# Down product of three middle groups of the second FFN: 2x2 block products made of seven, with the partial outputs in HBM

## The chip, the cores and the metric

The kernel runs on one core of a Trainium2 chip. TensorE (PE) multiplies and writes its sums into PSUM, eight banks of 128 partitions by 512 float32. VectorE (DVE) and ScalarE (ACT) read PSUM and SBUF; GpSimd (POOL) computes on SBUF and issues transfers; SyncE (SP) issues transfers. Each engine works its own queue in order, and engines wait for each other by semaphores.

The metric is device time in microseconds (us). Before the change it is 884.45 us, the median of three runs (884.32 to 885.13).

## The reference

One decoder layer on 512 tokens of width 1024, all float32: a half-step SwiGLU feed-forward layer (FFN), a mixer of a gated recurrence and sliding-window attention, and a second FFN, each between two RMS norms. The change concerns the second FFN:

```python
def swiglu(x, w_gu, w_down):
    gate, up = jnp.split(x @ w_gu, 2, axis=-1)
    return (jax.nn.silu(gate) * up) @ w_down
...
    x = x + 0.5 * rms_norm(swiglu(rms_norm(x, ffn2_pre_g[l]), ffn2_w_gu[l], ffn2_w_down[l]), ffn2_post_g[l])
```

`w_gu` is 1024 x 5632 (gate and up, 2816 columns each) and `w_down` is 2816 x 1024.

## The kernel before

**Numbers.** To keep float32 accuracy, each operand of a product is split into a rounded high part (`F32R`) and the rest, the low part. A product is three matmuls: high x high, high x low, low x high. For a weight block, ACT casts the high part (`act.copy`) and DVE subtracts it from the block to get the low part (`dve.tensor_sub`). Such a pair of tiles is a *unit*.

**Weights.** The class `Weights` holds the list of all loads and units in the order in which PE uses them. Raw weights are loaded by SP into three rotating buffers of 1 MB (`NRAW`), and units go into six rotating pairs (`NWS`). `take()` is called when PE is about to use a unit; it first issues the low parts, and the next cast, of units up to four ahead (`AHEAD`), then runs whatever was put off with `later(n, ...)` to the n-th take from then. So the place of every ACT and DVE instruction in its queue follows from the order of the calls; the schedule is manual, and nothing reorders it. When the last unit of a raw buffer has been split, the next load is issued.

**The second FFN.** The 2816 hidden features are 22 blocks of 128, in the groups `GROUPS2` = (0, 6), (6, 10), (10, 14), (14, 18), (18, 22). For each group the hidden values are computed (gate and up products, SiLU, multiplication), and then the down product of that group, whose result is added to `parts`, eight tiles of 128 tokens x 512 output columns in SBUF. The first group's gate and up products are plain (`classic`). From block 6 on two blocks at a time are made by `quad`: gate and up weights and the halves of the input form 2x2 blocks, whose product is done with seven half-size products instead of eight (the weight combinations are made by DVE in place in the raw buffer, `combine` in `add_quad`; the input's were made once, in `Next.sums`). Each of the seven takes one unit and is 24 matmuls of 128x256. `quad` ends with a SiLU of the gate half (`g1`), a multiplication, and `low_parts`, which splits the hidden values into high and low.

**The down product before** (line 1430 on): for each half `dh` of the output columns and each block f of the group, four token blocks `tb` times three matmuls of 128x512 (`mm3_out`, L1425 to L1427): 96 matmuls per middle group, from four units of 1024 elements per partition. DVE then adds each of the eight banks into `parts` (L1446). In the first group ACT copies the banks into `parts` (L1444).

**The last group** is done token block by token block: its down product is added to `parts`, the squares are summed, and the post-norm and the residual follow (from L1464). POOL multiplies by the gain there (L1495). Between the first group's hidden values and this, POOL has no work.

**Buffers.** SBUF tiles of 2 KB per partition come from one pool of 44 (`t2k`), short-lived ones from a pool of 8 (`wt`), PSUM banks from a pool of 8. A tile that reuses a buffer waits for the last reader of the former one.

Of the kernel before, what the change touches and what calls it, by code (L numbers as in the profile page):

```python
# [32 lines left out]
CLASSIC1, CLASSIC2 = 4, 6  # L33
PUMPS = [(2, 1)] * 8 + [(1, 1), (1, 0), (4, 0)]
# [77 lines left out]
def tile_layer(ctx: ExitStack, tc: tile.TileContext, out: bass.AP, **ins: bass.AP):  # L112
# [8 lines left out]
    psum = ctx.enter_context(tc.tile_pool(name="psum", bufs=8, space=bass.MemoryType.PSUM))  # L121
    E = mybir.EngineType
# [3 lines left out]
    HALF = [slice(0, T // 2), slice(T // 2, T)]  # L126

# [3 lines left out]
    def t2k(name, dt=F32):  # L131
        return big.tile([P, T], dt, tag="t2k", name=name, bufs=NT2K)
# [140 lines left out]

    for f0, f1 in GROUPS2:
        for f in range(f0, f1, 2):
            (add_gate_up if f < CLASSIC2 else add_quad)(w2, f, "b")
        if f1 < FC:
            for dh in range(2):
                for f in range(f0, f1, 4):
                    add_down(f, min(4, f1 - f), dh)  # L280
        else:
            for f in range(f0, f1, 4):
                for dh in range(2):
                    add_down(f, min(4, f1 - f), dh)
# [353 lines left out]
    class Hidden:  # L638
# [24 lines left out]
        def quad(self, f, last, ahead):  # L663
# [3 lines left out]
            hs = [(t2k(f"hh{n}{j}", F32R), t2k(f"hl{n}{j}", F32R)) for j in range(2)]  # L667
# [10 lines left out]
            def low_parts(x, h):  # L678
                for j in range(2):
                    act.copy(hs[j][0][:, HALF[h]], x[:, HALF[j]])  # L680
                for j in range(2):
                    hh, hl = hs[j]
                    dve.tensor_sub(hl[:, HALF[h]], x[:, HALF[j]], hh.bitcast(F32)[:, HALF[h]])
# [5 lines left out]
            p1, p7, u2, u4, g1 = (wt(f"{s}{n}") for s in ("p1", "p7", "u2", "u4", "g1"))  # L689
            seven(A, "b11", True)  # L690
            act.copy(p1, A)
# [4 lines left out]
            seven(B, "b21", True)  # L696
            dve.tensor_add(p1, p1, B)  # L697
            W.later(1, act.activation, p1, p1, AF.Silu)
# [15 lines left out]
            for j in range(2):  # L714
                self.hs[f + j] = hs[j]
# [35 lines left out]
        def chunks(self, f0, f1, ahead=AHEAD):  # L751
            for f in range(f0, f1, 2):
                self.quad(f, f == f1 - 2, ahead if f == f1 - 2 else AHEAD)
            return [self.hs.pop(f) for f in range(f0, f1)]

# [673 lines left out]
    parts = {}  # L1429
    for g, (f0, f1) in enumerate(GROUPS2[:-1]):  # L1430
        hs = hid.chunks(f0, f1) if g else hid.classic(f1, banks, {3: [(n2.sums, 0)], 3.5: [(n2.lows, 0)], 4.5: [(n2.sums, 1)], 5: [(n2.lows, 1)]}, AHEAD - 1)
        for dh in range(2):
            ybanks = [bank(f"yb{g}{dh}{tb}") for tb in range(NB)]
            for f in range(f0, f1):
                if f % 2 == 0:
                    w = W.take()
                for tb in range(NB):
                    mm3_out(ybanks[tb], hs[f - f0], tb, w, f % 2, ALL, f == f0, f == f1 - 1)
                if g == 0 and (dh, f) in ((0, 0), (0, 2), (1, 2), (1, 4)):
                    (n2.sums if f == 2 * dh else n2.lows)(2 + dh)  # L1440
            for tb in range(NB):
                if g == 0:
                    parts[tb, dh] = t2k(f"yp_b{tb}{dh}")
                    act.copy(parts[tb, dh], ybanks[tb])  # L1444
                else:
                    dve.tensor_add(parts[tb, dh], ybanks[tb], parts[tb, dh])  # L1446
    f0, f1 = GROUPS2[-1]
    hs = hid.chunks(f0, f1, ahead=5)
# [15 lines left out]
    for tb in range(NB):  # L1464
# [8 lines left out]
        for i, f in steps:  # L1473
# [12 lines left out]
            if f == f1 - 1:  # L1486
                y = parts[tb, dh][:, c0:c1]
                dve.tensor_add(y, banks[i][:, :c1 - c0], y)
# [52 lines left out]
```

## Time and profile before

| what | us or share |
|---|---|
| runs, median of three | 884.45 |
| profiled execution | 886.26, span 884.6 from first to last instruction, granted clock 0.997 |
| PE busy | 873.8 (99%) |
| DVE, ACT, POOL busy | 668.5 (76%), 459.5 (52%), 129.0 (15%) |
| one middle group, gate and up products (626.20 to 666.50) | 40.30 |
| the same group's down product (666.50 to 688.29) | 21.79 |
| HBM read, written | 83.67 MB, 2.10 MB |

The profile is one execution, recorded by the hardware profiler. A group of instructions is shown as line, engine, operation, out<-in, partitions x elements, count, and then busy time, the mean duration in ns, and the idle time of the engine just before them with what ended it. The chain of waits follows the work that ended last back to what released each step. A timeline row is start, length, engine, line, operation. PE's durations overlap, since matmuls are pipelined: the spacing of their starts is what they cost. The same holds in a smaller degree for DVE and ACT.

### The profile page before, as it was taken

To read this page: it belongs to the slowest core of one execution; us is meant where nothing else is said; L and a number is where in the kernel's file an instruction comes from. 1 tells how busy PE (TensorE), PEld (TensorE's weight loads), DVE (VectorE), ACT (ScalarE), POOL (GpSimd) and SP (SyncE) were. 2 spreads that over 40 slices of the span, in tenths; PEclk is the share of its full clock that TensorE was granted. 3 is DMA by queue.
4 is the path that set the end of the run, shared out by engine and by line. 5 is a ranking of instruction groups with operands and counts; after the bars stand their busy time and mean duration, and the time that the engine had idled before them with its cause. 6 is when DMAs were issued, how large, how long until landed. Compare 5 with 4: busy or idle time off the path is not lost.

```text
span 884.6 us, 14243 instructions
## 1 busy us (share of the span) xinstructions
PE 873.8 (99%) x5768; PEld 801.5 (91%) x5768; DVE 668.5 (76%) x993; ACT 459.5 (52%) x791; POOL 129.0 (15%) x117
## 2 busy tenths in 40 slices
PE   8999999999999999999999999999999999999997
PEld 8988999989989998998887899888998998998996
DVE  4979758778778864889999679588677677777754
ACT  6646534544535554457787346535463452552542
POOL 2010000000000015435463154210000000000013
PEclk9999999999999999999999999999999999999999
DMA  7242243152242253332301130224232241261212
GB/s 240 73 152 83 92 142 103 54 162 72 73 142 97 84 167 96 96 96 76 115 1 49 60 131 5 93 95 143 96 127 65 96 145 46 96 190 37 86 46 96
DMA packets 83553, 86.68 MB, mean 98 GB/s; under 512 B 3664, under 2 KB 75680, under 8 KB 83488
## 3 DMA queue, kind: packets, MB, share of 16 engines
q1 hardware_dynamic: 83312, 85.64, 30.2%
q8 instruction: 45, 0.74, 0.3%
q14 instruction: 20, 0.16, 0.1%
q10 hardware_dynamic: 144, 0.13, 0.0%
q0 software_dynamic: 32, 0.00, 0.0%
HBM read 83.67 MB, written 2.10 MB: 97 GB/s over the span
## 4 chain that ended last, share of the span: by engine, by line
PE 91%; DVE 5%; ACT 2%; issue 1%; DMA 1%; POOL 0%; SPq 0%; POOLq 0%; DVEq 0%; ACTq 0%
PE aa L676 12%; PE ab L676 10%; PE da L676 6%; PE db L676 5%; PE ya L361 4%; PE ya L362 4%; PE ya L363 4%; PE yb L1426 4%; PE yb L1427 4%; PE yb L1425 4%; PE ba L676 3%; PE bb L676 3%; PE a_first L841 1%; PE an L380 1%; PE mn L380 1%; PE mn L387 1%
## 5 line engine op out<-in xcount | busy, mean ns | idle before, releaser
L361 PE MATMUL ya<-hha,whi_ad 128*128 128x512 f32 x158 | 61.5, 389 | 0.0
L362 PE MATMUL ya<-hla,whi_ad 128*128 128x512 f32 x158 | 61.5, 389 | 0.0
L363 PE MATMUL ya<-hha,wlo_ad 128*128 128x512 f32 x158 | 61.5, 389 | 0.0
L1425 PE MATMUL yb<-whi_bd,hhb 128*128 128x512 f32 x144 | 56.1, 389 | 0.0
L1426 PE MATMUL yb<-wlo_bd,hhb 128*128 128x512 f32 x144 | 56.1, 389 | 0.0
L1427 PE MATMUL yb<-whi_bd,hlb 128*128 128x512 f32 x144 | 56.0, 389 | 0.0
L1495 POOL TENSOR_TENSOR yp_b<-yp_b,grow 128x512 f32<-128x512 f32 (+1 forms) x8 | 9.7, 1222 | 282.0 <-ACT ysq L1489 282.0
L942 POOL MEMSET bd_w_rg<- 128x512 f32 x1 | 0.5, 528 | 266.0 <-PE aa L676 266.0
L363 PEld LDWEIGHTS ya<-hha,wlo_ad 128*128 128x128 f32 x158 | 29.7, 188 | 6.2
L361 PEld LDWEIGHTS ya<-hha,whi_ad 128*128 128x128 f32 x158 | 29.7, 188 | 6.1
L362 PEld LDWEIGHTS ya<-hla,whi_ad 128*128 128x128 f32 x158 | 29.7, 188 | 6.0
L1427 PEld LDWEIGHTS yb<-whi_bd,hlb 128*128 128x128 f32 x144 | 27.0, 188 | 5.6
L1425 PEld LDWEIGHTS yb<-whi_bd,hhb 128*128 128x128 f32 x144 | 27.0, 188 | 5.6
L1426 PEld LDWEIGHTS yb<-wlo_bd,hhb 128*128 128x128 f32 x144 | 27.0, 188 | 5.5
L176 DVE TENSOR_TENSOR wlo_bd<-raw_bd,whi_bd 128x1024 fp32r<-128x1024 f32 x22 | 26.4, 1219 | 3.6 <-ACT whi_bd L171 3.6
L171 ACT CAST whi_bd<-raw_bd 128x1024 fp32r<-128x1024 f32 x22 | 22.9, 1049 | 5.1 <-PE bb L676 3.8
L1446 DVE TENSOR_TENSOR yp_b<-yb,yp_b 128x512 f32<-128x512 f32 x24 | 16.4, 692 | 11.6 <-PE yb L1427 11.6
L1000 DVE TENSOR_TENSOR yp_a<-ya,yp_a 128x512 f32<-128x512 f32 x24 | 16.4, 686 | 8.8 <-PE ya L363 8.8
L697 DVE TENSOR_TENSOR p1a<-p1a,ba 128x512 f32<-128x512 f32 x9 | 6.2, 688 | 21.7 <-PE ba L676 21.7
L697 DVE TENSOR_TENSOR p1b<-p1b,bb 128x512 f32<-128x512 f32 x8 | 5.5, 688 | 18.2 <-PE bb L676 18.2
L380 PE MATMUL an<-xh_mx,whi_xl 128*128 128x256 f32 x64 | 15.9, 289 | 0.0
L381 PE MATMUL an<-xh_mx,wlo_xl 128*128 128x256 f32 x64 | 15.5, 283 | 0.0
(1523 smaller groups left out, 3418.4 us busy)
## 6 DMA issues: line engine op xcount, KB each, us to landing
raw_bd<-in_ffn_w_down SPq DMA_DIRECT2D x10, 1024.0 KB, 6.8
xn<-in_x SPq DMA_DIRECT2D x8, 256.0 KB, 4.6
raw_q<-in_w_in SPq DMA_DIRECT2D x4, 512.0 KB, 3.8
out_dram<-yp_b SPq DMA_DIRECT2D x7, 256.0 KB, 2.0
first<-in_ffn_w_gu SPq DMA_DIRECT2D x4, 256.0 KB, 5.1
raw_second<-in_ffn_w_gu SPq DMA_DIRECT2D x2, 512.0 KB
raw_ag__104<-in_ffn_w_gu SPq DMA_DIRECT2D x1, 1024.0 KB
raw_au__286<-in_ffn_w_gu SPq DMA_DIRECT2D x1, 1024.0 KB, 5.8
```

The source lines that it names most:

```text
L171: act.copy(two(hi, x), x)
L176: low.tensor_sub(two(lo, x), x, two(hi.bitcast(F32), x))
L361: pe.matmul(ps, hi[:, k, :], xh, start=start, stop=False)
L362: pe.matmul(ps, hi[:, k, :], xl, start=False, stop=False)
L363: pe.matmul(ps, lo[:, k, :], xh, start=False, stop=stop)
L380: pe.matmul(ps[:, sl], hi[:, k, :], xh, start=k == 0, stop=False)
L676: pe.matmul(o, w[:, k, js], x, start=first and i + j + k == 0, stop=k == 3 and i == 2, skip_group_check=True)
L1000: dve.tensor_add(parts[c], b, parts[c])
L1425: pe.matmul(ps, hh[:, blk], hi[:, k, cs], start=start, stop=False)
L1426: pe.matmul(ps, hh[:, blk], lo[:, k, cs], start=False, stop=False)
L1427: pe.matmul(ps, hl_[:, blk], hi[:, k, cs], start=False, stop=stop)
L1446: dve.tensor_add(parts[tb, dh], ybanks[tb], parts[tb, dh])
```

## The change

For the three middle groups, blocks 6 to 17 (`SEVEN_DOWN = 6, 18`), the down product is done with 2x2 blocks too. The hidden values of a group are 512 tokens x 512 features; the left factor's four blocks are token halves x feature pairs, the right factor's are feature pairs x column halves. Seven products of the blocks' sums and differences take the place of eight:

- *Weights* (`add_seven_down`): two loads of 1 MB with whole rows of `w_down`, and seven units of 1024 elements; four of them are combinations that DVE makes in place.
- *Hidden values* (`seven_left`, `seven_right`, `form`): instead of eight splits of 256 columns, seven forms of 512: blocks a11, a12, a22 and the combinations s1 to s4. The forms are made as soon as `quad` has the halves, some put off to later takes.
- *Products* (`seven_down`): seven times 12 matmuls of 128x512, 84 per group, in pairs of banks A, B, D, E. After the first product ACT copies A into B, and the third product accumulates on that copy.
- *Output* (`to_parts`): `parts` are now eight tiles in HBM. ACT copies a bank into a staging tile, and POOL issues a transfer that adds it to one or two of the parts: 12 copies and 14 transfers of 256 KB per group. The first group's result is copied to staging (negated for the right half) and stored by POOL. Before the last group's gate and up products POOL issues the loads of the eight parts into SBUF; the right half is subtracted at the end, since its sign is turned.
- *All quads*: bank A is copied by ACT into bank B, and the fourth product accumulates there, instead of a copy into `p1` and an addition by DVE.

```diff
+SEVEN_DOWN = 6, 18
...
+    def add_seven_down(f):
+        wd = ins["ffn2_w_down"]
+        rx, ry = (W.raw(lambda i=i: load_raw([wd[0, (f + i) * P:(f + i + 2) * P, :]], 2, D, f"b{'xy'[i // 2]}d{f}_")) for i in (0, 2))
+        left, right = HALF_D
+        b11, b12, b21, b22 = (rx, left), (rx, right), (ry, left), (ry, right)
...
+        unit(b11, "p")
+        unit(b12, "q", combine(dve.tensor_add, b12, b22, b12))
+        unit(b21, "r")
+        unit(b12, "s", combine(dve.tensor_add, b12, b12, b11))
+        unit(b21, "t", combine(dve.tensor_add, b21, b12, b21))
+        unit(b11, "u", combine(dve.tensor_sub, b11, b12, b22))
+        unit(b22, "v")
...
+        def form(self, name, x):
+            hh, hl = t2k(f"hh{name}", F32R), t2k(f"hl{name}", F32R)
+            act.copy(hh, x)
+            dve.tensor_sub(hl, x, hh.bitcast(F32))
+            self.forms[name] = hh, hl
+
+        def seven_left(self, f, x, second):
+            self.blocks[second, 0] = x
+            self.form("a12" if second else "a11", x)
+
+        def seven_right(self, f, x, second):
+            self.blocks[second, 1] = x
+            a11, a21 = self.blocks[0, 0], self.blocks[0, 1]
+            if not second:
+                s3 = wt(f"s3{self.name}{f}")
+                dve.tensor_sub(s3, a11, a21)
+                self.form("s3", s3)
+                return
+            a12, a22 = self.blocks[1, 0], x
+            s1, s2, s4 = (wt(f"{s}{self.name}{f}") for s in ("s1", "s2", "s4"))
+            dve.tensor_sub(s1, a22, a21)
+            dve.scalar_tensor_tensor(s2, s1, -1.0, a11, op0=ALU.mult, op1=ALU.subtract)
+            self.form("s2", s2)
+            W.later(1, self.form, "a22", a22)
+            W.later(2, self.form, "s1", s1)
+            W.later(3, dve.scalar_tensor_tensor, s4, s2, -1.0, a12, ALU.mult, ALU.subtract)
+            W.later(3, self.form, "s4", s4)
...
             seven(A, "b11", True)
-            act.copy(p1, A)
+            act.copy(B, A)
...
-            seven(B, "b21", True)
-            dve.tensor_add(p1, p1, B)
-            W.later(1, act.activation, p1, p1, AF.Silu)
+            seven(B, "b21", False)
+            W.later(1, act.activation, p1, B, AF.Silu)
...
+    parts = {(tb, dh): hbm.tile([P, T], F32, name=f"yp_b{tb}{dh}") for tb in range(NB) for dh in range(2)}
+
+    def seven_down(f):
+        forms = hid.seven_forms(f)
+        A, B, Dd, E_ = ([bank(f"y{s}{f}{i}") for i in range(2)] for s in "abde")
+
+        def seven(banks, form, first, stop):
+            w = hi, lo = W.take()
+            hh, hl_ = forms[form]
+            for i in range(2):
+                for k in range(2):
+                    js = slice(k * (T // 2) + i * P, k * (T // 2) + (i + 1) * P)
+                    pe.matmul(banks[i], hh[:, js], hi[:, k, :], start=first and k == 0, stop=False, skip_group_check=True)
+                    pe.matmul(banks[i], hh[:, js], lo[:, k, :], start=False, stop=False, skip_group_check=True)
+                    pe.matmul(banks[i], hl_[:, js], hi[:, k, :], start=False, stop=k == 1, skip_group_check=True)
+
+        def to_parts(banks, *blocks):
+            for i in range(2):
+                st = t2k("stage")
+                act.copy(st, banks[i])
+                for tb, dh in blocks:
+                    pool.dma_start(parts[2 * tb + i, dh], st, accum_op=ALU.add)
+
+        seven(A, "a11", True, True)
+        for i in range(2):
+            act.copy(B[i], A[i])
+        seven(Dd, "s3", True, True)
+        to_parts(Dd, (1, 1))
+        seven(B, "a12", False, True)
+        to_parts(B, (0, 0))
+        seven(A, "s2", False, True)
+        to_parts(A, (1, 0))
+        seven(Dd, "a22", False, True)
+        to_parts(Dd, (1, 0))
+        seven(A, "s1", False, True)
+        to_parts(A, (1, 1), (0, 1))
+        seven(E_, "s4", True, True)
+        to_parts(E_, (0, 1))
...
-                if g == 0:
-                    parts[tb, dh] = t2k(f"yp_b{tb}{dh}")
-                    act.copy(parts[tb, dh], ybanks[tb])
-                else:
-                    dve.tensor_add(parts[tb, dh], ybanks[tb], parts[tb, dh])
+                st = t2k("stage")
+                act.activation(st, ybanks[tb], AF.Copy, scale=-1.0 if dh else 1.0)
+                pool.dma_start(parts[tb, dh], st)
...
+    in_hbm, parts = parts, {}
+    for tb in range(NB):
+        for dh in range(2):
+            parts[tb, dh] = t2k(f"yp_b{tb}{dh}")
+            pool.dma_start(parts[tb, dh], in_hbm[tb, dh])
...
-                dve.tensor_add(y, banks[i][:, :c1 - c0], y)
+                (dve.tensor_sub if dh else dve.tensor_add)(y, banks[i][:, :c1 - c0], y)
```

## The prediction

> **What bounds the kernel now.** I read the page's busy shares and its chain first, then the stage table and the chain in order of time around the second group, then the timelines of ScalarE (ACT) and VectorE (DVE) where its down product begins. The page:
>
> ```profile
> PE 873.8 (99%) x5768; PEld 801.5 (91%) x5768; DVE 668.5 (76%) x993; ACT 459.5 (52%) x791; POOL 129.0 (15%) x117
> ...
> PE 91%; DVE 5%; ACT 2%; issue 1%; DMA 1%; POOL 0%; SPq 0%; POOLq 0%; DVEq 0%; ACTq 0%
> ...
> L176 DVE TENSOR_TENSOR wlo_bd<-raw_bd,whi_bd 128x1024 fp32r<-128x1024 f32 x22 | 26.4, 1219 | 3.6 <-ACT whi_bd L171 3.6
> L171 ACT CAST whi_bd<-raw_bd 128x1024 fp32r<-128x1024 f32 x22 | 22.9, 1049 | 5.1 <-PE bb L676 3.8
> L1446 DVE TENSOR_TENSOR yp_b<-yb,yp_b 128x512 f32<-128x512 f32 x24 | 16.4, 692 | 11.6 <-PE yb L1427 11.6
> ```
>
> TensorE (PE) is busy throughout and carries the chain; DVE follows at 76%. In the changed stages the margin is this (columns: stretch, length, busy time of PE, PEld, DVE, ACT, POOL, clock, DMA share, GB/s):
>
> ```profile
> 626.20:666.50 40.30, 40.30 (x337) 40.30 (x337) 27.42 (x32) 22.62 (x32) 0.00 (x0) 1.00 0.40 131
> 666.50:688.29 21.79, 21.79 (x99) 18.02 (x98) 15.92 (x20) 5.53 (x7) 0.00 (x0) 1.00 0.16 49
> ```
>
> One middle group is 14 gate/up products of 2.88 us, then 21.8 us of down product, with no hole in PE. A group takes 62.10 us (626.19 to 688.29), the same in all three, by the chain in order of time (start, length):
>
> ```profile
> 626.19 2.87 PE ab L676 x24
> ...
> 688.29 2.87 PE ab L676 x24
> ```
>  In the down stage ACT is nearly free. What matters is what stands at the seam:
>
> ```profile
> 663.66 0.69 DVE L703 TENSOR_TENSOR u2b<-u2b,db 128x512 f32<-128x512 f32 x1 [1.57 <-PE db L676]
> 664.38 0.69 DVE L704 TENSOR_TENSOR u2b<-p1b,u2b 128x512 f32<-128x512 f32 x1
> 664.99 1.22 DVE L176 TENSOR_TENSOR wlo_bd<-raw_bd,whi_bd 128x1024 fp32r<-128x1024 f32 x1
> ```
> ```profile
> 666.34 0.40 PE L1425 MATMUL yb<-whi_bd,hhb 128*128 128x512 f32 x1
> 666.58 0.40 PE L1426 MATMUL yb<-wlo_bd,hhb 128*128 128x512 f32 x1
> ```
> ```profile
> 666.54 0.60 ACT L707 ACTIVATE g1b<-ab 128x512 f32<-128x512 f32 x1 [0.72 <-PE ab L676]
> 667.90 0.72 ACT L680 CAST hhb<-g1b 128x256 fp32r<-128x256 f32 x2 [0.76 <-DVE g1b L686]
> 671.46 1.05 ACT L211 CAST whi_bq__7151<-raw_bx__7041 128x1024 fp32r<-128x1024 f32 x1 [2.84 <-DVE raw_bx__7041 L220]
> ```
>
> Here DVE's last work of the quad starts 0.2 us after PE ends its sixth product (663.46), and ACT's last SiLU 0.2 us after the seventh (666.34). The third line shows an ACT cast of a combined weight block: it stands idle until DVE's combination is done, and everything behind it in ACT's queue stands too.
>
> **Part 1, the matmuls.** 96 of 128x512 per group become 84. They issue every 0.227 us (21.79/96), so 12 fewer save 2.72 us, 8.16 us over three groups. All of it lies on PE's chain.
>
> **Part 2, ACT and DVE in total.** Per group ACT gains 3 casts of 1024 (1.05), 12 copies to staging and 2 from bank A to bank B (0.59 each, row L1444: 592 ns), and 7 casts of 512 (0.62) for 8 of 256: 28.15 to about 41 us. DVE gains 3 subtractions of 1024 and 4 combinations (1.22 each), 7 low parts of 512 (0.68) for 8 of 256, and s1 to s4 (0.7), and loses 8 additions of L1446 and 2 of L697: 43.34 to about 49.5. Ideal group length is 62.10 - 2.72 = 59.4, so neither is the bound as a total. The order decides.
>
> **Part 3, the order at the seam.** In the changed program's ACT queue the first copy from A to B stands behind: cast of down unit t, cast of a12, SiLU, cast of s2, cast of unit u, cast of a22. PE's third product, a12, accumulates into B and cannot start before that copy. I lay the queues out from 663.66 in the old trace's clock, with rows' durations and their spacings (DVE 1024: next 1.14 later; ACT 1024: 0.95, 512: 0.53; hand-over 0.03 to 0.09):
> - DVE: the two u2 steps 663.66 and 664.38, low of unit s 664.99, combination b21 666.13 to 667.35.
> - ACT: cast t 667.44, cast a12 668.39, SiLU 668.92 to 669.52 (it ran at 666.54 before).
> - DVE: low of a12 669.04, g1 times u4 669.65, s1 670.37, s2 671.09 to 671.83 (0.74, the L482 form).
> - ACT: cast s2 671.87 to 672.49.
> - DVE: low s2 672.52, low of unit t 673.13, combination u 674.27 to 675.49.
> - ACT: cast u 675.58, cast a22 676.53, copy to B 677.06 to 677.65; PE at 677.70.
>
> PE would have wanted it at 666.34 + 5.44 = 671.78: a hole of **5.9 us**. Every step from the sixth product on is a measured row and none waits for a transfer.
>
> A second hole is of the same kind. The sixth product, s1, accumulates into A and needs ACT's staging copy of A, queued behind the cast of the next quad's unit q, which waits for its combination. ACT: second B copy 677.54, cast v 678.02, cast s1 678.97 to 679.59. DVE: low s1 679.62, low v 680.23, s4 681.37 to 682.11. ACT casts s4 682.15 to 682.77; DVE: low s4 682.80, low p 683.41, combination q 684.55 to 685.77; ACT: cast q 685.86, copy of A 686.81 to 687.40. PE wanted it at 677.70 + 3 x 2.72 = 685.86 and gets it at 687.45: **1.6 us**. The next quad finds its first A copy done some 2 us ahead of its third product, so I see no third hole.
>
> **Part 4, the transfers from GpSimd.** Per group 14 accumulating transfers of 256 KB, plus 8 stores after group 0 and 8 loads before the last. POOL has nothing else between 587 and 857 us, so its own waits (the second addition into one part waits for the first to land) hold only further transfers. But ACT waits too: the staging copy after a22 reuses the buffer of the first one. That one leaves ACT at 680.1, is issued in 0.72 us (the one POOL transfer of the old trace) and must land by about 690.3, with 2 us of slack behind: 11.5 us in all. No row shows an accumulating transfer. The nearest are in the page's list of transfers (last column: median us to landing):
>
> ```profile
> raw_bd<-in_ffn_w_down SPq DMA_DIRECT2D x10, 1024.0 KB, 6.8
> xn<-in_x SPq DMA_DIRECT2D x8, 256.0 KB, 4.6
> ...
> out_dram<-yp_b SPq DMA_DIRECT2D x7, 256.0 KB, 2.0
> ```
>
> So 2.0 us below and, as an addition reads its stage and its target and writes the target, three times 256 KB, 6.8 us above; I take 6, nearest to the large load, and cost it at nothing, since 11.5 covers both ends. The Trainium skill (DMA: Bandwidth & Descriptors, Anatomy of one DMA) gives a GpSimd-issued transfer about 2.0 us plus its bytes at 436 GB/s; by that the estimate is 2.6 us, and the sum stays the same.
>
> The 8 loads are queued 40 us ahead of their first use, the last quads' 40.3 us. SP loads the same bytes per group; buffers come free later: the next quad's second half would be issued at about 679.1 and land by 685.8 (5.8 us for 1 MB), needed at 688.1. Cover 2.3 us, and if it is gone the excess is lost in each group.
>
> **Part 5, the rest.** In all 17 quads ACT copies A into B instead of into p1 (same 0.59) and the DVE addition of 0.69 goes. B is needed three products (8.6 us) after the copy can begin, so PE gains and loses nothing; DVE was not the bound there. After group 0 ACT still makes 8 copies of 0.59, now into staging, and stores follow that nothing waits for until group two's first additions, over 40 us later; the subtraction at the end costs what the addition did. Cost: nothing.
>
> **Sum.** -8.16 + 3 x (5.9 + 1.6) = **+14.3 us**. The profiled execution took 886.26 (span 884.6), 0.2% above the median of 884.45; its span would be 898.9. On the median's scale: **898.7 us**, 1.6% slower.
>
> **Rivals.**
> 1. *The holes don't open, the matmuls' gain stays* (other sign). For: ACT at 5.53 of 21.79 us in the old down stage, and totals that fit. Against: the queue order. It decides at 2.72 us of holes per group, so B's copy would have to be done by about 674.4, before the combination of u has even started. Time 884.45 - 8.2 = 876.3.
> 2. *Accumulating transfers land late.* Past 11.5 us ACT stands, and each microsecond costs one per group; 13.5 us gives 6 more, 905. Against: 1 MB in 6.8 us.
> 3. *GpSimd's issuing slows DVE.* For: beside a POOL tensor operation at 576.6 one DVE subtraction took 1.79 us instead of 0.68. Four issues of 0.72 fall into the second chain: 0 to 2.9 us per group, 0 to 8.6 in all; half of it gives 903. The Trainium skill (SBUF — State Buffer, Who interferes with whom) says a DVE instruction with two SBUF inputs contends with GpSimd's reads, not its writes, and that descriptor writing left such instructions alone. The row agrees on reads; by the page this term is nothing.
>
> **Numbers.** The two holes as laid out, 894 to 902: 0.70. Late transfers: 0.10. Slowed DVE: 0.12. Holes only partly open, near no net change: 0.03, a third of it on the faster side. No holes: 0.05. Row spacings may be off by a tenth over an 11 us chain, 1.1 us per group, which is the 894. Low end 891 for partly covered holes; high 908 for rivals 2 and 3. A change under 0.2% can't be told from none; faster 0.06, same 0.02, slower 0.92.
>
> **What would show it.** Three idle stretches of PE of 5 to 6 us ahead of yb with ACT's copy into yb as releaser, three of 1 to 2 us ahead of ya with the staging copy; PE near 97% of the span; a middle group of 66.9 us instead of 62.1. ACT waits at whi_bdu for DVE's combination. Wrong if PE shows no hole at yb, if ACT's staging copies are released by transfers, or if additions land beyond 11 us.

## The result, and the profile after

The changed kernel takes **911.70 us**, the median of four runs (910.15 to 912.47), against 884.39 us for the kernel before beside it: a ratio of 1.0305, 95% interval 1.0287 to 1.0323. It is 3.1% slower. The forecast was 898.7 us, range 891 to 908: the sign was right, the time lies 3.7 us above the range.

The page of the changed kernel, the lines that answer to those of before (busy time by engine, the queue of GpSimd's transfers, the chain):

```profile
PE 876.4 (96%) x5732; PEld 802.4 (88%) x5732; DVE 681.1 (75%) x982; ACT 490.5 (54%) x839; POOL 174.3 (19%) x175
...
q0 software_dynamic: 7360, 15.21, 8.5%
...
PE 82%; DVE 9%; ACT 3%; issue 2%; DMA 2%; POOL 0%; SPq 0%; POOLq 0%; DVEq 0%; ACTq 0%
```

PE has 36 matmuls less and yet is busy 2.6 us longer, in a span that is 25.8 us longer (910.4). So some of its matmuls run slower, and 4% of the span is idle. The waits of PE name the holes, the stretches in which it stands idle (total us, times, longest):

```profile
PE yb L1521 <- ACT yb L1534: 17.0, 3, 5.7
PE ab L744 <- ACT u4b L771: 3.8, 2, 2.0
```

The stage table has the rest (columns as before: stretch, length, busy time of PE, PEld, DVE, ACT, POOL, clock, DMA share, GB/s). Rows one and two are the second group, which stood at 40.30 and 21.79 us before; then the fourth group's gate and up products, its down product, and the last group's gate and up products:

```profile
626.05:666.35 40.30, 40.30 (x338) 40.30 (x337) 29.11 (x30) 20.82 (x27) 1.24 (x3) 1.00 0.40 132
666.35:692.98 26.63, 20.98 (x87) 16.85 (x86) 18.92 (x21) 16.07 (x26) 5.24 (x6) 0.87 0.52 125
...
760.46:804.50 44.04, 42.07 (x338) 41.87 (x337) 31.60 (x33) 21.71 (x29) 6.93 (x8) 0.96 0.63 150
804.50:831.74 27.24, 21.59 (x85) 17.34 (x84) 19.52 (x21) 16.70 (x26) 5.20 (x6) 0.87 0.54 127
831.74:875.74 44.00, 42.22 (x338) 42.01 (x337) 28.87 (x33) 22.30 (x33) 11.29 (x16) 0.96 0.72 185
```

The down product takes 26.6 us and its clock is 0.87: the groups are 66.93, 67.48 and 71.28 us long, against 62.10. Two stages of gate and up products, which the change hardly touches, are 3.7 us longer, also at a lower clock; the two before them, of 40.30 us and (third group, not shown) 40.29 us, are not.

**The seam.** ACT's and PE's timeline where the second group's down product begins (start, length, engine, line, operation, and in brackets the idle time before it and its releaser):

```profile
668.25 0.61 ACT L704 CAST hha<-u2b 128x512 fp32r<-128x512 f32 x1
668.77 0.59 ACT L778 ACTIVATE g1b<-ab 128x512 f32<-128x512 f32 x1
671.68 0.62 ACT L704 CAST hhs<-s2b 128x512 fp32r<-128x512 f32 x1 [2.32 <-DVE s2b L724]
675.38 1.04 ACT L291 CAST whi_bdu__7158<-raw_bxd__6916 128x1024 fp32r<-128x1024 f32 x1 [3.08 <-DVE raw_bxd__6916 L300]
676.33 0.61 ACT L704 CAST hha<-g1b 128x512 fp32r<-128x512 f32 x1
676.85 1.06 ACT L1534 COPY yb<-ya 128x512 f32<-128x512 f32 x2
```
```profile
677.48 0.79 PE L1521 MATMUL yb<-whi_bdr__7043,hha 128*128 128x512 f32 x1 [5.65 <-ACT yb L1534]
678.08 0.63 PE L1522 MATMUL yb<-wlo_bdr__7044,hha 128*128 128x512 f32 x1
678.50 0.63 PE L1523 MATMUL yb<-whi_bdr__7043,hla 128*128 128x512 f32 x1
```

This is the laid-out queue: the cast of u at 675.38 (forecast 675.58), the copy at 676.85 (677.06), PE at 677.48 (677.70). But the matmuls after the hole start every 0.43 us instead of 0.227, at about half rate. That had not been forecast, and the second hole, ahead of ya, is not there at all.

**The late holes.** The two others lie in the stages of 44 us. SP issues a weight load at 763.07 while five additions into `parts` go out, and the combination that needs it waits until 776.29:

```profile
763.07 1.08 SPq L149 DMA_DIRECT2D raw_by__8054<-in_ffn_w_gu  x2
...
763.31 4.37 POOL L1530 DMA_DIRECT2D yp_b<-stage  x5 [0.83 <-ACT whi_bu__7996 L214]
...
776.29 1.23 DVE L223 TENSOR_TENSOR raw_bx__7993<-raw_by__8054,raw_bx__7993 128x1024 f32<-128x1024 f32 x1 [3.73 <-DMA raw_by__8054<-in_ffn_w_gu]
...
779.70 0.53 PE L744 MATMUL ab<-b2h_f,whi_bv__8025 128*128 128x256 f32 x1 [1.97 <-ACT u4b L771]
```

The load took 13.2 us. ACT's cast of the combined block and, behind it in the queue, the copies that PE waits for come after it; and this hole too is followed by 3.4 us of matmuls at half rate (48 matmuls in 7.51 us instead of 5.76). In the third group the same load went out at 696.15, 0.8 us ahead of the lot of five, and its combination started at 705.20 without a wait for it: there no hole opened. The other late load went out 0.3 us behind the start of such a lot.

### The profile page after: what moved, and what is told of

Same layout as the page of the kernel before. It is cut to its first block, busy times and chain, and to the rows that moved or that the text cites. A ratio compares the mean times of both kernels' runs of the same rounds, so it can differ in the third digit from the quotient of the medians.

```text
span 910.4 us, 14407 instructions
## 1 busy us (share of the span) xinstructions
PE 876.4 (96%) x5732; PEld 802.4 (88%) x5732; DVE 681.1 (75%) x982; ACT 490.5 (54%) x839; POOL 174.3 (19%) x175
## 4 chain that ended last, share of the span: by engine, by line
PE 82%; DVE 9%; ACT 3%; issue 2%; DMA 2%; POOL 0%; SPq 0%; POOLq 0%; DVEq 0%; ACTq 0%
PE aa L744 11%; PE ab L744 9%; PE da L744 6%; PE db L744 4%; PE ya L400 4%; PE ya L401 4%; PE ya L399 4%; PE ba L744 3%; PE bb L744 2%; PE a_first L920 1%; DMA raw_by__8726<-in_ffn_w_gu 1%; PE yb L1505 1%; PE yb L1504 1%; PE yb L1506 1%; PE an L418 1%
## 5 line engine op out<-in xcount | busy, mean ns | idle before, releaser
L1530 POOL DMA_DIRECT2D yp_b<-stage x42 | 36.4, 1168 | 186.2 <-ACT stage L1528 139.1
L1505 PE MATMUL yb<-wlo_bd,hhb 128*128 128x512 f32 x48 | 18.7, 389 | 0.0
L1504 PE MATMUL yb<-whi_bd,hhb 128*128 128x512 f32 x48 | 18.7, 389 | 0.0
L1506 PE MATMUL yb<-whi_bd,hlb 128*128 128x512 f32 x48 | 18.7, 389 | 0.0
L565 POOL TENSOR_TENSOR acca_r<-acca_r,sq_r 128x512 f32<-128x512 f32 x6 | 8.5, 1410 | 48.1 <-ACT sq_r L430 48.1
L179 DVE TENSOR_TENSOR wlo_bd<-raw_bd,whi_bd 128x1024 fp32r<-128x1024 f32 x10 | 12.1, 1222 | 7.0 <-ACT whi_bd L174 7.0
L399 PE MATMUL gt<-xh_mx,whi_gt 128*128 128x512 f32 x32 | 14.2, 443 | 0.0
L692 POOL TENSOR_TENSOR usb<-usb,gsb 128x512 f32<-128x512 f32 x5 | 7.7, 1539 | 33.0 <-DVE usb L689 21.8
L1504 PE MATMUL ybl<-whi_bd,hhb 128*128 128x512 f32 (+1 forms) x36 | 13.5, 375 | 0.0
L1505 PE MATMUL ybl<-wlo_bd,hhb 128*128 128x512 f32 (+1 forms) x36 | 13.2, 366 | 0.0
```

The costliest lines, as they stand in the source:

```text
L179: low.tensor_sub(two(lo, x), x, two(hi.bitcast(F32), x))
L399: pe.matmul(ps, hi[:, k, :], xh, start=start, stop=False)
L1504: pe.matmul(ps, hh[:, blk], hi[:, k, cs], start=start, stop=False)
L1505: pe.matmul(ps, hh[:, blk], lo[:, k, cs], start=False, stop=False)
L1506: pe.matmul(ps, hl_[:, blk], hi[:, k, cs], start=False, stop=stop)
L1530: pool.dma_start(parts[2 * tb + i, dh], st, accum_op=ALU.add)
```

## Experiments

A table first; "before" is the kernel before, run beside each (884.4 to 885.9 us). no_adds, reordered_no_adds and spin_no_adds leave the middle groups' additions out, and plain_stores stores in place of adding: these four do not compute the full output and only show where time goes.

| kernel | us | ratio to before, 95% interval |
|---|---|---|
| changed kernel | 911.70 | 1.0305 (1.0287 to 1.0323) |
| no_adds | 901.76 | 1.0198 (1.0182 to 1.0213) |
| plain_stores | 903.43 | 1.0217 (1.0200 to 1.0234) |
| spin | 906.24 | 1.0241 (1.0224 to 1.0259) |
| evac_first | 911.48 | 1.0310 (1.0279 to 1.0340) |
| reordered_no_adds | 881.39 | 0.9964 (0.9954 to 0.9974) |
| reordered | 904.91 | 1.0224 (1.0195 to 1.0253) |
| summed | 904.28 | 1.0225 (1.0205 to 1.0245) |
| spin_no_adds | 899.85 | 1.0176 (1.0159 to 1.0193) |
| paced | 885.83 | 1.0005 (0.9993 to 1.0017) |
| after_paced | 903.88 | 1.0203 (1.0188 to 1.0218) |
| paced_copy | 885.26 | 0.9999 (0.9988 to 1.0010) |
| paced_copy_644 | 884.69 | 0.9993 (0.9984 to 1.0002) |

### What do the transfers cost: no_adds, plain_stores

```diff
 # no_adds
-                for tb, dh in blocks:
-                    pool.dma_start(parts[2 * tb + i, dh], st, accum_op=ALU.add)
 # plain_stores
-                    pool.dma_start(parts[2 * tb + i, dh], st, accum_op=ALU.add)
+                    pool.dma_start(parts[2 * tb + i, dh], st)
```

> Leaves out the 42 accumulating transfers of the three middle groups (the staging copies of ScalarE stay; the 8 plain stores of the first group and the 8 loads back stay), so the output lacks the middle groups' share of the down product. Theory 1: the forecast priced the transfers at nothing, and that was the failed step: while they are in flight SP's weight loads land late (1 MB in 13 us instead of 6 to 7), a combination of VectorE waits for one, and the cast of ScalarE behind it opens the two holes of 1.97 and 1.78 us ahead of bank A's matmuls at 779.70 and 850.96, each followed by some 1.7 us of matmuls at half rate. Without them these two holes are gone, the three groups take 66.9 to 67.5 us each, the last quads 40.3 instead of 44.0, and the time falls by 7 to 9 us to 903 to 905; 900 to 902 if the 2.6 us that the end has grown by also come from the additions. The hole of 5.7 us ahead of the third product stays in all three groups. Rival: the two late holes come from the order of ScalarE's and VectorE's queues, as the first hole does; then nothing changes, 910 to 912. A third way: GpSimd's issuing itself slows VectorE; then VectorE's 128x512 subtractions and additions get shorter in the down stage (mean of the stage's VectorE instruction, 0.90 us now).

> The 42 accumulating transfers become plain stores to the same places (accum_op left out), so each part in HBM holds the last product stored and not the sum. Same number of transfers, same bytes written, no read of what was there. Theory 1a: it is the reading and adding that makes the transfers long (256 KB in 7.4 us median, 9 and more when several are out; out_dram<-yp_b lands 256 KB in 2.0) and keeps the weight loads late; then plain stores land in 2 to 4 us, the two late holes go, and the time is that of the kernel without the transfers, 901 to 905. Theory 1b: any transfer of this size in that stretch delays the loads; then the late holes stay, 908 to 912. Between them, 905 to 908, if a part of the delay goes.

Without the additions the time falls by 9.9 us, to 901.76: theory 1. PE's holes ahead of yb are the same 17.0 us in three, the late ones are gone, and the last quads take 40.3 us. Plain stores of the same bytes give nearly the same, 903.43; the 1.7 us between the two are mostly the end of the program (4.3 us behind GpSimd's last instruction without the additions, 5.7 with stores or additions). The lists of transfers and queues from 600 to 900 us, of the changed kernel, of plain_stores and of no_adds (packets, MB, share of 16 engines; then count, KB and median us to landing):

```profile
q0 software_dynamic: 7328, 15.21, 25.8%
...
yp_b<-stage POOLq DMA_DIRECT2D x50, 256.0 KB, 7.4
...
raw_bxd__8220<-in_ffn_w_down SPq DMA_DIRECT2D x1, 1024.0 KB, 13.1
...
raw_by__8726<-in_ffn_w_gu SPq DMA_DIRECT2D x2, 512.0 KB, 7.7
```
```profile
q0 software_dynamic: 4640, 15.21, 13.2%
...
yp_b<-stage POOLq DMA_DIRECT2D x50, 256.0 KB, 3.8
...
raw_bxd__8220<-in_ffn_w_down SPq DMA_DIRECT2D x1, 1024.0 KB, 9.1
...
raw_by__8726<-in_ffn_w_gu SPq DMA_DIRECT2D x2, 512.0 KB, 4.4
```
```profile
q0 software_dynamic: 1280, 4.20, 4.0%
...
raw_bxd__8192<-in_ffn_w_down SPq DMA_DIRECT2D x1, 1024.0 KB, 4.9
...
raw_by__8684<-in_ffn_w_gu SPq DMA_DIRECT2D x2, 512.0 KB, 4.0
```

With the 4.0% of the stores and loads that no_adds keeps taken off, 42 additions hold 21.8% of 16 x 300 us, 25 us of one DMA engine each; as plain stores they hold 9.2%, 10.5 us. So it is mainly the addition, not the bytes, that makes the weight half in these rows land in 7.7 us instead of 4.0 (4.4 beside stores). Stores are not free either: the load of 1 MB lands in 13.1 us beside additions, 9.1 beside stores and 4.9 without; beside stores that opened no hole. GpSimd's issuing is not it: plain_stores issues as many.

In no_adds the groups take 66.81, 67.41 and 67.78 us. Their hole is 5.65 us each time; what differs is how long PE runs at half rate behind it: 3.1, 4.7 and 5.3 us by the spacing of its matmuls (the last section shows why).

### Why no second hole: spin, spin_no_adds

```diff
+SPIN = 24
...
         to_parts(Dd, (1, 1))
+        hh = forms["s3"][0]
+        for _ in range(SPIN):
+            pe.matmul(E_[0], hh[:, :P], hh, start=True, stop=True, skip_group_check=True)
         seven(B, "a12", False, True)
```

> Adds 24 matmuls of 128x512 per group between the second and the third product, from s3's form into a bank that the last product clears later: 24 x 0.227 = 5.4 us of work without use, in place of the hole of 5.7 us. Nothing else is changed. Theory: the second hole of the forecast (1.6 us ahead of ya) did not open only because the clock fell in the first hole: the matmuls after it ran at half rate for 3.4 us, which delayed PE by 1.7 us and gave ScalarE that time. With PE kept busy the third product takes 2.72 us instead of 4.39, a hole of 1.5 to 2.0 us opens ahead of ya, and the time stays within 2 us of the changed kernel's, 910 to 914 (to 917 if that hole also costs the clock). Rival: the second hole was a mistake of the forecast's layout; then nothing opens and the time falls by 3 x 1.7 = 5 us to 906 to 907.

> The 24 matmuls without use of the run before, and no accumulating transfers (the output lacks the middle groups' share). With transfers these matmuls gained 5.5 us, though the second group kept its length (66.84 us against 66.93), its hole of 5.7 us turned into work and one of 1.16 us opened ahead of ya. Theory: the gain was in the late weight loads alone (one late hole in that profile and not two); without transfers there are none, so the time is that of the kernel without transfers, 901.8 within 1.5 us. Rival: keeping the clock up is worth 1.7 us per group in itself: 896 to 898.

PE's waits in spin: the hole of 5.65 us is work now, and a hole ahead of ya has opened, as laid out, only smaller (1.16 us; forecast 1.6):

```profile
676.19 0.50 PE L1522 MATMUL yb<-whi_bdr__7043,hha 128*128 128x512 f32 x1 [0.21 <-ACT yb L1535]
...
685.84 0.50 PE L1522 MATMUL ya<-whi_bdu__7158,hhs 128*128 128x512 f32 x1 [1.16 <-ACT stage L1529]
```

The second group keeps its length, 66.84 us against 66.93, so here the slow matmuls after the first hole had only taken the second hole's place. The time, though, fell by 5.5 us, to 906.24, which by the expectation spoke for the rival. The traces say from where: one late hole (1.92 us, at full clock) in place of two with half rate behind them. spin_no_adds settles it: 899.85, 1.9 us below no_adds; the rival had asked for 896 to 898, the theory for 900.3 at the least, so this is a little outside the theory too. The three groups are now 66.84 us each. The clock is worth nothing in the second group, and 0.6 and 0.9 us in the two whose half-rate stretch was longer; the end is 0.8 us shorter as well.

### Is it the order of ACT's queue: evac_first, reordered_no_adds, reordered

evac_first issues the copies out of a product's banks before the work for the next units; the reordered kernels also swap the products s4 and s1 and their units u and v:

```diff
-        def seven(banks, form, first, stop):
-            w = hi, lo = W.take()
+        def seven(banks, form, first, stop, then=None):
+            hi, lo = W.ready[W.taken] if then else W.take()
...
+            if then:
+                then()
+                W.take()
...
+        def copy_first():
+            for i in range(2):
+                act.copy(B[i], A[i])
+            hid.form("s2", hid.s2)
-        seven(A, "a11", True, True)
-        for i in range(2):
-            act.copy(B[i], A[i])
+        seven(A, "a11", True, True, copy_first)
...
 # reordered
-        unit(b11, "u", combine(dve.tensor_sub, b11, b12, b22))
-        unit(b22, "v")
+        unit(b22, "v", combine(dve.tensor_sub, b11, b12, b22))
+        unit(b11, "u")
...
-            W.later(2, self.form, "s1", s1)
-            W.later(3, dve.scalar_tensor_tensor, s4, s2, -1.0, a12, ALU.mult, ALU.subtract)
-            W.later(3, self.form, "s4", s4)
+            dve.scalar_tensor_tensor(s4, s2, -1.0, a12, op0=ALU.mult, op1=ALU.subtract)
+            W.later(2, self.form, "s4", s4)
+            W.later(3, self.form, "s1", s1)
```

> Only the order in which ScalarE's work is issued in the down product changes: after a product's matmuls the copies out of its bank (bank A to B, bank to staging) come ahead of the casts, combinations and low parts for the next weight units, and the copy from A to B comes ahead of the form of s2; all work and all transfers stay. Theory: the place of the copies in ScalarE's queue makes the first hole. Then the holes of 5.7 us ahead of yb are gone with their half-rate stretch (7.5 us per group), and the layout gives a next hole of 2.8 us ahead of ya (the copy of A to staging behind the second product's work), with 1.7 us of half rate after it: 3 x (7.5 - 4.5) = 9 us faster than the changed kernel, 902 to 905, still above the kernel before. Rival: ScalarE and VectorE are late in total after the quads, whatever the order; then the hole moves to the next product with about its size, and the time is 908 to 912.

> The copies out of the banks first, as in the run before; beside that the products come in the order a11, s3, a12, s2, a22, s4, s1 (s1 last, so that bank A's staging copy has two products of cover), s4 is computed with s1 and s2, and its form and that of s1 come two and three takes later. The 42 accumulating transfers are left out, so the output lacks the middle groups' share. Theory: with the seam's order mended and no transfers, what is left is the gain of the matmuls, 8.2 us, less holes of 1.1 us per group ahead of the next quad's third product, plus 1.2 us at the end (the end grew from 3.1 to 4.3 us with the 16 transfers that stay): 884.9 - 8.2 + 3.3 + 1.2 = 881, between 879 and 884. Rival: VectorE and ScalarE, with 12 and 19 us of added work per group, are late in total whatever the order; then the groups stay near 66 us and the time above 895.

> The same order with all 42 accumulating transfers: the full computation. Theory: the transfers hold the DMA engines in the down stage (the slices of the engines' busy share there read 9 of 10, against 6 to 8 without the transfers or with plain stores), so the next quad's weights are late as they were when only the copies were moved (loads of 12 to 13 us, holes of 4 to 5 us ahead of the next quad's third product in each group and half rate after them): 881 + 3 x 6.5 + 1.4 at the end = 900 to 903. Rival: the late loads belonged to the old order's bunching; then 882 to 886, and the transfers cost nothing as forecast.

evac_first missed: 911.48, no gain. The hole ahead of yb is gone, but others are there (waits of PE):

```profile
PE ab L744 <- ACT bb L763: 12.7, 3, 5.3
PE ya L1521 <- ACT stage L1531: 7.6, 3, 2.5
```

The 2.5 us ahead of ya are the laid-out 2.8. The other kind is new, and its chain in order of time begins with a load:

```profile
677.67 12.78 DMA raw_by__7227<-in_ffn_w_gu
690.54 1.24 DVE raw_bx__7198 L223
```

PE is no longer late itself, so it needs the next quad's weights earlier, and they come as late as the additions let them. Without the additions the mended order gives what it should: reordered_no_adds takes 881.39 us (expected 881), 0.36% below the kernel before. All that PE waits for in the changed stages is 3.7 us, with no clock lost:

```profile
PE ab L744 <- ACT bb L763: 3.7, 3, 1.2
```

That is the -8.2 us of the matmuls with 3.7 and some small change given back. With the additions the same order takes 904.91, 23.5 us more (expected 900 to 903): holes of 3.37, 5.67 and 5.20 us behind loads of 9.3 to 11.6 us. So the two troubles hide each other: against the changed kernel the order alone brings 0.2 us (evac_first) or 6.8 (reordered), leaving the additions out alone 9.9, both together 30.3.

### Fewer transfers: summed

Pairs of products for the same part are added in SBUF by GpSimd; 8 additions leave per group instead of 14.

```diff
+        def add(x, y):
+            for i in range(2):
+                pool.tensor_add(x[i], x[i], y[i])
...
+        def after_a22():
+            x = staged(Dd)
+            add(x, sums["u2"])
+            send(x, (1, 0))
```

> The reordered kernel, but pairs of products that go to the same part are added in SBUF first, by GpSimd (6 additions of 128x512 per group), so that 8 accumulating transfers leave per group and not 14. The full computation. Theory: the engine time of the transfers per group falls by 6 of 14, from 22 to 12.5 us of all 16 engines, and the weight loads come sooner; holes of 0 to 2 us per group: 882 to 892, and faster than the reordered kernel by at least 8 us. Rival 1: the additions on GpSimd slow VectorE, whose down-stage operations then get longer than 0.7 (512 columns) and 1.22 us (1024) by 10% or more; 890 to 900. Rival 2: any accumulation at the group's end is too late for the next quad's load; then as the reordered kernel.

904.28: no better than reordered, and past the 890 to 900 of rival 1, but by rival 1's mechanism. GpSimd's and DVE's timelines:

```profile
688.96 4.40 POOL L1543 TENSOR_TENSOR stage<-stage 128x512 f32<-128x512 f32 x2 [0.74 <-ACT stage L1532]
...
694.46 3.15 POOL L1543 TENSOR_TENSOR stage<-stage 128x512 f32<-128x512 f32 x2
```
```profile
690.03 2.18 DVE L223 TENSOR_TENSOR raw_by__7226<-raw_by__7226,raw_bx__7197 128x1024 f32<-128x1024 f32 x1
692.13 2.31 DVE L218 TENSOR_TENSOR wlo_bt__7330<-raw_bx__7197,whi_bt__7329 128x1024 fp32r<-128x1024 f32 x1
694.37 4.33 DVE L218 TENSOR_TENSOR wlo_bu__7345<-raw_by__7226,whi_bu__7344 128x1024 fp32r<-128x1024 f32 x1
698.63 1.21 DVE L218 TENSOR_TENSOR wlo_bv__7374<-raw_by__7226,whi_bv__7373 128x1024 fp32r<-128x1024 f32 x1
```

DVE's 1.22 us become 2.2 to 4.3 beside GpSimd's additions, and DVE's chain opens holes of 4.4 to 4.6 us ahead of the seventh product of the next quad instead, with 2.2 to 2.3 us ahead of the third. Behind the second and third group's down product the chain of waits into these holes holds no load; behind the fourth's it has one of 9.8 us, so there a late load has a part. The Trainium skill (SBUF — State Buffer, Who interferes with whom) says that a DVE instruction with two SBUF inputs contends with GpSimd instructions that read SBUF; this trace agrees.

### Transfers out of the loads' way: paced, after_paced

The staged blocks wait; GpSimd reads one column of a weight tile, so that it stands until that load has landed, and then sends a lot.

```diff
+    def gate(raw, n):
+        def run(tile):
+            for i, fn in enumerate(W.pending[:n]):
+                if not i:
+                    pool.tensor_copy(small.tile([P, 1], F32, tag="tick", name=f"tick{raw}"), tile[:, 0, :1])
+                fn()
+            del W.pending[:n]
+        W.gates[raw] = run
...
-                    pool.dma_start(parts[2 * tb + i, dh], st, accum_op=ALU.add)
+                    W.pending.append(lambda o=parts[2 * tb + i, dh], st=st: pool.dma_start(o, st, accum_op=ALU.add))
```

> The reordered kernel with all 42 accumulating transfers, but none leaves in the down stage: the staged blocks wait in SBUF, and GpSimd sends 5, 6 and 3 of a group's 14 after it has read one column of a weight tile, which it can do only when that tile's load has landed (the first load of the group's second quad, that of the down product's first half, and the first of the next group), so that they run in stretches in which no weight load is out. The loads of the parts back move behind the last quads. The full computation. Theory: the transfers cost only by their collision with the weight loads; paced, the late holes are gone, the groups take the 60.9 us of the reordered kernel without transfers, and the end has its 5.7 us (3.1 before): 881.4 + 1.4 = 883, between 881 and 888, which is just below the kernel before. Rival: accumulating transfers slow VectorE, ScalarE or later loads wherever they run; then 892 and more.

> The changed kernel in its own order of products and copies, with the transfers paced in the same way: the two of s3 leave at once, the other 12 of a group in two lots of 6, after the loads named before have landed. The full computation. Theory: only the collisions go, so the time is that of the kernel without transfers, with 1.4 us more at its end: 903, between 901 and 906, with the holes of 5.7 us ahead of yb kept and none of the two late ones. Rival: as in the paced kernel; then 908 to 912, no gain.

after_paced takes 903.88 us (expected 903), with all 42 additions and the old order: 7.8 us come back by moving them. paced takes 885.83 (expected 883, 881 to 888), 19 us less than reordered, and as much as the kernel before. GpSimd's timeline shows the lots between the loads:

```profile
682.79 0.85 POOL L151 COPY tick<-raw_bx__7327 128x1 f32<-128x1 f32 x1 [56.41 <-DMA raw_bx__7327<-in_ffn_w_gu]
683.58 4.41 POOL L1555 DMA_DIRECT2D yp_b<-stage  x5
701.22 0.18 POOL L151 COPY tick<-raw_bxd__7561 128x1 f32<-128x1 f32 x1 [13.23 <-DMA raw_bxd__7561<-in_ffn_w_down]
701.69 4.35 POOL L1555 DMA_DIRECT2D yp_b<-stage  x5 [0.28 <-issue]
```

PE waits 4.6 us ahead of ab in the three stages (1.2, 1.2 and 2.2), at full clock, and the end is 2.6 us longer than before; -8.2 + 4.6 + 2.6 = -1.0 us, against -1.5 in the profiled spans (883.1 and 884.6) and -0.1 in the medians (885.83 and 885.89).

### Can it beat the kernel before: paced_copy, paced_copy_644

```diff
-            seven(A, "b11", True)
-            act.copy(B, A)
+            seven(A, "b11", True, then=(lambda: act.copy(B, A)) if f > 6 and self.name == "b" else None)
+            if f <= 6 or self.name != "b":
+                act.copy(B, A)
```

> The paced kernel (same pacing, 5, 6 and 3 transfers), and in the quads from the second middle group on the copy from bank A to bank B is issued right behind the first product, ahead of the casts for the next weight units. The full computation. Theory: this takes away the holes of 1.2 us (2.2 in the last) ahead of each quad's third product, where ScalarE's copy stood behind three casts: 885.8 - 3 to 4.5 = 881 to 883, faster than before by 0.2 to 0.5%. Rival: VectorE and ScalarE are close to their limit there, and the hole moves to the next bank (p7, u2 or u4): 884 to 887.

> As the last kernel, but a group's transfers leave in lots of 6, 4 and 4. The full computation. In the paced kernel the second lot (6, behind the down product's first load) still ran when the next load went out, which took 8.0 us in place of some 5. Theory: a shorter second lot mends that: 0.5 to 2 us faster than the last kernel. Rival: the first lot of 6 then meets the load of the quad's second half; no difference, within 1 us.

885.26 and 884.69: neither can be told from the kernel before. In paced_copy the holes ahead of the third product shrink from 4.6 to 2.9 us in all, and 1.7 us of waits for the copy into u4 take their place, two of the four behind loads of 9.0 and 6.8 us: the rival. The shorter second lot gives 0.6 us, at the edge of what was expected and within the runs' spread. No version here beats the kernel before with the full computation.

## Why the prediction was wrong, step by step

The sum by steps, all in the profiled executions' spans (884.6 and 910.4), for three groups and what follows:

| step | forecast | measured |
|---|---|---|
| 36 matmuls fewer | -8.2 | -8.2 |
| hole ahead of yb | 17.7 | 17.0 (3 x 5.65) |
| second hole, ahead of ya | 4.8 | none |
| half rate after the first hole | 0 | 6.9 (1.9, 2.5, 2.5) |
| accumulating transfers | 0 | 7.4 (holes of 1.97 and 1.78, and the half rate after them) |
| end, behind GpSimd's last instruction | 0 | 2.6 |
| sum | 14.3 | 25.7 |

The half-rate entry is what a group's excess over 62.10 us leaves after the matmuls and the hole; the late holes are the excess of the two stages of 44 us over 40.3. The medians differ by 27.3 us and the spans by 25.8, since the profiled execution of the kernel before was 1.8 us above its median.

- **The mechanism of the slowdown was right.** The layout of the seam's queues, row by row, gave PE's start in the second group to 0.22 us, and the hole is 5.65 us in all three. Without the transfers the kernel takes 901.76 us, 3.1 us from the forecast. That closeness is partly luck: 4.8 us had been counted for a second hole that did not open, and the half rate, not counted, took 6.9 in the changed kernel.
- **The step that failed is the price of the accumulating transfers**, "cost it at nothing, since 11.5 covers both ends". The landing time was taken as 6 us, between 2.0 and 6.8 (2.6 by the estimate beside it); the median was 7.4. Of the 42 additions eight, all in lots of five, landed after more than 11 us, the latest after 14.8, which the prediction had named as a sign of being wrong. But that delay alone cost nothing on PE's chain: the additions that the reasoning was about, the first of each group, landed in 5.6 to 6.7 us, and no staging copy waited for one. I looked only at who waits for the transfer; the price of 7.4 us lay with who shares the DMA engines with it. The text came near, "cover 2.3 us, and if it is gone the excess is lost in each group", with the 5.8 us of a quiet load, for the next quad's second half. That load, issued at 678.87, was in time. Late was the second half of the quad behind it: 13.2 us beside five additions.
- **The second hole was mis-sized by a cause ahead of it.** Its chain was right (spin shows it, 1.16 us), but it starts from PE's time, and PE was delayed by the clock. The clock after a hole of 5.9 us was no term of the sum; it cost 2.1 us more than the forecast had for the hole it replaced.
- **The end** was no term either. From GpSimd's last instruction to the end of the span: 3.1 us with one GpSimd transfer in the program, 3.3, 3.5 and 4.3 with 17, 4.2 with 41, 5.7 with 59, stores and additions alike. In the traces GpSimd ends with a DRAIN instruction, of 0.91 us with one transfer, 2.23 with 17, 4.19 with 41 and 5.66 with 59, some 0.08 us for each; with 41 and more it is all of that end. Why the DRAIN grows was not tried.
- Rival 1, 876.3, did not happen; reordered_no_adds comes nearest to it, 881.4, in another order and without the additions. Rival 2 did not happen as told: ACT's staging copies wait for no transfer (two of its casts do, for 0.7 and 0.8 us, and PE stood idle behind neither); POOL waits for its own (30.8 us in five waits, 9.1 the longest). Rival 3 did not happen: DVE's operations of 1024 elements keep their 1.22 us in the changed kernel.
- The copy into B in all quads, with which "PE gains and loses nothing", held: the second group's gate and up products take 40.30 us in both kernels, and start at 626.05 against 626.19.

## What to carry to other kernels

A transfer that nobody waits for still has a price: look at which loads are out in the same stretch, and take their duration under it, not from a quiet stretch. Such a transfer can be moved behind a load by making its engine read one column of what the load brings. And when a schedule has two limits at one place, here a queue's order and late weights, taking one away shows less than it is worth (6.8 and 9.9 us alone, 30.3 together); try each with the other removed.

## What the runs showed of the hardware that I had not expected

- **TensorE's clock after a hole.** Counted over all kernels here, in the stages from 620 to 875 us: after 21 of 21 holes of 3.1 us and more the granted clock fell to about 0.5; after 16 of 16 holes of 0.9 to 1.7 us it stayed at 1.00; between, from 1.78 to 2.54 us, it fell after 3 of 10. What decides is where the hole lies, for in these traces the clock switches only on a grid of 3.41 us. In the changed kernel it falls at 673.97, 742.24, 779.78, 813.92 and 851.47; the distances between these times are 20, 11, 10 and 11 times 3.413, and it returns after 3.41 or 6.83 us. One step of that grid and the next, in the changed kernel and then in spin (grid counted from its switch at 896.53), whose hole of 1.92 us lies across a step's end (columns as before, the clock ahead of the last two):

```profile
776.37:779.78 3.41, 1.44 (x13) 1.24 (x11) 2.22 (x2) 2.15 (x4) 0.85 (x1) 1.00 0.96 189
779.78:783.20 3.42, 3.42 (x16) 3.42 (x17) 3.39 (x6) 2.03 (x3) 0.85 (x1) 0.50 0.45 47
...
773.66:777.07 3.41, 2.04 (x17) 1.83 (x16) 1.67 (x2) 1.52 (x3) 0.86 (x1) 1.00 1.06 305
777.07:780.49 3.42, 2.87 (x24) 2.87 (x25) 3.39 (x5) 2.50 (x4) 0.85 (x1) 1.00 0.79 140
```

  The hole of 1.97 us lies whole in one step, PE is busy for 1.44 us of it, and the clock is 0.50 in the next. In spin PE is busy for 2.04 and 2.87 us, and the clock stays. Over all kernels here, between 40 and 880 us, 1.97 us or more of idle time within a step at full clock brought the drop at its end each time, up to 1.58 us never, and 1.79 us once in two. So the half rate behind a hole of 5.65 us lasts until a step ends, 3.0 to 5.8 us in 12 cases, and a hole of 2 us can cost 3.7. The Trainium skill (TensorE: Matmul & The Clock Gate, Part 1: The HAM clock gate) puts the drop at one idle window of about 3.4 us, and the return after about as much busy time. The length of the window agrees; but a window that was idle for 1.97 us, or once 1.79, was enough here.
- **An addition into HBM costs the DMA engines 2.4 times a plain store** of the same 256 KB (25 against 10.5 us of one engine, 7.4 against 3.8 us to landing), and slowed two loads of SP's queue, from 4.0 to 7.7 us (512 KB) and from 4.9 to 13.1 (1 MB).
